# A copy inside SBUF in the first turn of GpSimd's DMA queue, and one DMA engine's rows spread in eighths

## Chip, cores and metric

The kernel runs on one core of one Trainium2 chip. The metric is the device time of one execution in microseconds (us); several executions of a kernel are given by their median, lowest and highest. A profiled execution also has a span, from its first to its last instruction. The core has a tensor engine (PE, which reads its weights as PEld), a vector engine (DVE), a scalar engine (ACT), GpSimd (POOL) and SyncE (SP), and 16 DMA engines, numbered 0 to 15 here. SP and POOL issue this kernel's transfers; SP's go through queue q1, POOL's through q0.

## The reference

```python
def reference(x, y):   # both (8, 12, 512, 64) float32
    return np.einsum('bhtc,bhsc->bhts', x, y).astype(np.float32)
```

For each of 96 pairs (batch, head) a 512 x 512 matrix is made as x times y transposed, over 64 channels. 25.17 MB are read and 100.66 MB written.

## The kernel before, in words

**Work and order.** The 96 pairs are taken in 6 groups of 16 (`NG`), each group in two halves (`NH` = 12). Inputs come in 2 MB loads (line 204), are turned into bf16 by ACT, DVE and POOL (lines 167 and 169), mixed into `xbs` (`mix`, line 232) and transposed in 32 x 32 blocks by DVE (`transposes`, lines 252 and 261). A half gives four *outputs* of 2 MB each (`V` = 4), 48 in all: 128 partitions of `N` = 4096 fp32 values, that is 16 KB a partition. In which order the four heads of a half are made is the list `heads` (line 157), here 0, 2, 1, 3; PE, ACT and the stores all follow it. For one output PE makes 8 products of 512 columns (line 275) into two PSUM tensors, ACT copies each to a slot in SBUF (line 167), and the slot is stored. Eight slots lie as four pairs.

**Stores.** Most stores take two outputs at once, 4 MB from a pair of slots, and are issued by SP (`store`, line 366, through `transfer`, line 184). Such a transfer is written as an access pattern of source and destination; the first count of the pattern is its outer one. SP issues each as soon as ACT has filled the slots, and the slots are filled again when the store has landed. The last output, 47, is copied out of PSUM by DVE.

**Output 44.** The first output of the last half (`SHARED` = 44) is stored in pieces. Its even partitions go with output 45's even ones in one 2 MB transfer of SP, output 45's odd ones in 1 MB behind it; outputs 46 and 47 are the last 4 MB of SP's queue. The odd partitions of output 44 are dealt out by `shares` (line 301). The code counts four partitions (so two odd rows) to a DMA engine in each of two blocks: with b = 0 or 1, engine e has the odd rows from 4e + 32b, for e above 7 from 32 more. `turns` (line 95) holds, as first engine and number of engines, (0, 5), (5, 3) and (8, 8). `odd` (line 304) issues the rows of k engines through `part` (line 293), which gives the source 2k rows and the destination the pattern (k, 2, columns).

- POOL issues, for b = 0 and then b = 1, the three turns. The rows of the first turn, engines 0 to 4, are cut: only columns 0 to `CUT[b]`, which are 512 (b = 0) and 1536 (b = 1) of the 4096; the others are whole.
- SP issues for engines 0 to 3 the columns from `CUT[b]` on, to the end with b = 0, to 1024 (`LEFT`) before the end with b = 1.
- What is left of these rows (of engine 4's, and the last 1024 columns of the rows of engines 0 to 4 with b = 1) is *made again*. `remade` (line 320) lists three pieces: columns 1536 to 3072 of engine 4's two rows of b = 1, cut in thirds for engines 13 to 15; the last 1024 columns of b = 1 of engines 0 to 4, whose ten rows lie on engines 8 to 12; and columns 512 to 4096 of engine 4's rows of b = 0 in eighths for engines 0 to 7. After its last product PE computes these pieces once more (`again`, line 330, matmuls on line 344), with the columns of the weights shifted so that a piece comes out on the partitions of the engines that are to store it; DVE copies them from PSUM to `xks[0]` and POOL issues three transfers (`rest`, line 351), in the order of their first engine.

So POOL's queue has, in this order, transfers with outer counts 5, 3, 8, 5, 3, 8 and, later, 8, 5, 3.

**Waits.** `emit` (line 140) gives every instruction the semaphore waits that its reads and writes need. Of POOL's transfers the first waits for ACT's copies of output 44, and the first of the made-again ones for DVE's copy.

Of the kernel before, what the change touches and what calls it, by code (L numbers as in the profile page):

```python
# [9 lines left out]
def kernel(  # L10
# [19 lines left out]
    _, _, S, _ = y.shape  # L30
    P = 128
# [10 lines left out]
    N = K * S  # L42
# [7 lines left out]
    while len(ROUNDS) < (V * NH - SINGLE) // 2:  # L50
        ROUNDS += [PAIRS - 1, *ROUND[LATE % 3:], *ROUND[:LATE % 3]]
    LAST = 2 * ROUNDS[(V * NH - SINGLE) // 2 - 1]
    CUT = [S, 3 * S]
    LEFT = 2 * S
    fp32 = mybir.dt.float32
    bf16 = mybir.dt.bfloat16
    u32 = mybir.dt.uint32
# [9 lines left out]
    def buffer(name, width, dtype):  # L67
        return nc.alloc_sbuf_tensor(name, [P, width], dtype)[:, :]
# [5 lines left out]
    def spare(g, lo, hi):  # L74

        return slots[SLOTS + g - 1][:, lo * N // 4:hi * N // 4]

    spares = range(1, 2 * PAIRS - SLOTS + 1)
    xks = [
        spare(g, 0, 2).bitcast(bf16) if g in spares else buffer(f"xk{g}", R * C, bf16)  # L80
        for g in range(NG - 1)
    ]
# [7 lines left out]
    xbs = [buffer(f"xb{half}", K * E * D, u32) for half in range(2)]  # L90
    xTs = [buffer(f"xT{i}", K * D * E, u32) for i in range(2)]
    yTs = [buffer(f"yT{i}", D * R // 2, u32) for i in range(2)]
    pms = [nc.alloc_psum_tensor(f"pm{i}", [P, 4, S], fp32)[:, :, :] for i in range(2)]

    turns = [(0, 5), (5, 3), (8, 8)]
    engines = {"act": nc.scalar, "dve": nc.vector, "pool": nc.gpsimd, "pe": nc.tensor, "sp": nc.sync}
# [3 lines left out]
    def need(name, points, told=True):  # L100

        best = {}
        for p, v in points:
            if known[name].get(p, 0) < v:
                best[p] = max(best.get(p, 0), v)
        for p, v in list(best.items()):
            if any(snaps[q, w].get(p, 0) >= v for q, w in best.items() if q != p):
                del best[p]
        for p, v in best.items():
            if told:  # L110
                engines[name].wait_ge(sems[p], v)  # L111
            known[name][p] = v
            for q, w in snaps[p, v].items():
                known[name][q] = max(known[name].get(q, 0), w)

    def promise(name, reads, writes):

        points = [writer[r] for r in (*reads, *writes) if r in writer]
        points += [v for w in writes for v in readers.get(w, ())]
        if name == "pool" and name in ticks:  # L120
            points.append((name, ticks[name]))
        return points

    def record(name, p, step, reads, writes, queue=False):
        at = (p, ticks.get(p, 0) + step)
        ticks[p] = at[1]
        if not queue:
            own[name][p] = at[1]
        snaps[at] = {**known[name], **own[name], p: at[1]}
        for r in reads:  # L130
            readers.setdefault(r, []).append(at)
        for w in writes:
            writer[w], readers[w] = at, []

    def signal(p):
        if p not in sems:
            sems[p] = nc.alloc_semaphore(p)
        return sems[p]

    def emit(name, make, reads=(), writes=(), dma=None, by=None, step=1):  # L140
        need(name, promise(name, reads, writes))
        p = by or name
        if dma is not None:
            p, step = f"dma{dma}", 16
        made = make().then_inc(signal(p), step)
        record(name, p, step, reads, writes, dma is not None)
        return made.ins.name
# [6 lines left out]

    places = [0, 4, 3, 1, 2, 0, 4, 3, 1, 2, 4, 3]
    first = [0, 1, 2, 4, 0, 1]
    heads = [0, 2, 1, 3]
    held = {
        SLOTS + g - 1: [[("xk", g)], [("yb", h, g, ch) for h in range(2) for ch in range(2)]]
        for g in spares  # L160
# [3 lines left out]
    def copy(name, dst, src, reads, writes, by=None):  # L164
        emit(
            name,
            lambda: nc.scalar.activation(dst, src, COPY)  # L167
            if name == "act"
            else engines[name].tensor_copy(dst, src),  # L169
            reads,  # L170
            writes,
            by=by,
        )

    def both(*ids):
        return [("slot", i, pm) for i in ids for pm in range(2)]

    def place(ap, pattern):
        name = ap.tensor.name
        return mybir.PhysicalAccessPattern(  # L180
            ap=pattern, offset=ap.offset, dtype=ap.dtype, memref=name, memsetref=f"{name}_set"
        )

    def transfer(name, dst, src, to=None, of=None):

        to = to or dst.ap
        of = of or [src.ap[0], *[[1, 1]] * (len(to) - len(src.ap)), *src.ap[1:]]
        return engines[name].add_instruction(  # L188
            mybir.InstDMACopy(
                name=nc.get_next_instruction_name(),  # L190
                engine=engines[name].engine,
                ins=[place(src, of)],
                outs=[place(dst, to)],
                mode="Copy",
                cce_op=mybir.AluOpType.bypass,
                queue={"sp": "qSPDynamicHW", "pool": "qPoolDynamic"}[name],
            )
        )
# [94 lines left out]
    def part(name, dst, src, k, reads, dma):  # L293

        assert src.ap[0][1] == 2 * k and dst.ap[0][1] == k
        emit(
            name, lambda: transfer(name, dst, src, dst.ap),
            reads=reads, dma=dma,
        )

    def shares(o, s):

        to, mine = ov[o // V, heads[o % V]], slots[s]
        def odd(name, b, e, k, lo, hi):

            p = 4 * e + 32 * b + (32 if e > 7 else 0)
            n = 2 * k
            dst = to[p // 2:p // 2 + n, 1, lo:hi].rearrange("(k i) n -> k i n", i=2)
            part(name, dst, mine[p + 1:p + 2 * n:2, lo:hi], k, both(s), "pool" if name == "pool" else s)

        for b in range(2):
            for e, k in turns:
                odd("pool", b, e, k, 0, N if e else CUT[b])
        for b in range(2):
            odd("sp", b, 0, 4, CUT[b], N - b * LEFT)

    remade = [  # L320
        (1, CUT[1], (N - LEFT - CUT[1]) // 3, 4, 13, 3, 0),
        (1, N - LEFT, LEFT, 20, 8, 5, 0),
        (0, CUT[0], (N - CUT[0]) // 8, 4, 0, 8, 0),
    ]

    def lies(e):

        return 4 * e + (32 if e > 7 else 0)
# [22 lines left out]
    def rest():  # L351

        half = SHARED // V % 2
        to = ov[SHARED // V, heads[SHARED % V]]
        top = lies(16)
        mine = xks[0][:top].bitcast(fp32)[:, :LEFT]
        emit("pe", again, [("xT", half), ("yT", half)], [("pm", 0)])
        copy("dve", mine, pms[0][:top, :LEFT // S].rearrange("p j s -> p (j s)"), [("pm", 0)], [("xk", 0)])
        for b, first, width, n, e, k, skip in sorted(remade, key=lambda r: r[4]):
            row, pieces = 16 * b + 10 - n // 2, 4 * k // n  # L360
            dst = to[row:row + n // 2, 1, first:first + pieces * width]
            dst = dst.rearrange("i (k n) -> k i n", k=k) if n == 4 else dst.rearrange("(k i) n -> k i n", k=k)
            p = lies(e)
            part("pool", dst, mine[p + 1:p + 4 * k:2, skip:skip + width], k, [("xk", 0)], "pool")

    def store(o):
        i, j = divmod(o, V)
        if o == SHARED:
            s = 2 * ROUNDS[(o - SINGLE) // 2]
            shares(o, s)  # L370
        elif o == SHARED + 1:
            n = ROUNDS[(o - SINGLE) // 2]
            emit(
                "sp", lambda: transfer("sp", ow[i, heads[j - 1]][:, :2], pairs[n][::2]),
                reads=both(2 * n, 2 * n + 1), dma=2 * n,
            )
            emit(
                "sp", lambda: transfer("sp", ov[i, heads[j]][:, 1], slots[2 * n + 1][1::2]),
                reads=both(2 * n + 1), dma=2 * n + 1,
            )  # L380
        elif o in ALONE:
            s = first[o]
            emit("sp", lambda: nc.sync.dma_start(ov[i, heads[j]], slots[s]), reads=both(s), dma=s)
        elif o % 2:
            n = first[o] // 2 if o < SINGLE else ROUNDS[(o - SINGLE) // 2]
            emit(
                "sp", lambda: transfer("sp", ow[i, heads[j - 1]], pairs[n]),
                reads=both(2 * n, 2 * n + 1), dma=2 * n,
            )
# [55 lines left out]
    for o in range(V, V * NH):  # L445
        result(o)
        if o % V == V - 1:
            prepare(o // V + 2)
    all_products()
    rest()  # L450
    emit("sp", nc.sync.nop)

# [35 lines left out]
```

## Time and profile before

| what | value |
|---|---|
| median of 3 runs | 297.85 us (297.57 to 297.97) |
| the profiled execution's own time | 298.19 us |
| its span | 296.4 us |
| PE, DVE, ACT, POOL busy | 45%, 53%, 69%, 22% of the span |
| moved by DMA, mean rate | 125.85 MB, 425 GB/s |
| landing of the last transfer | 296.29 us |

The profile is of one execution. Of its parts, the slices cut the span in 40 and give each engine's busy share in tenths; DMA in them is the mean of the 16 DMA engines. A line on DMA issues tells the destination and source, the issuing queue, how many, the size of each in KB and the median time from issue to landing. The trace under the page holds every DMA packet with its queue, start, length and size, but not its engine, and the moments at which each transfer's semaphore was incremented, 16 in all for a transfer. Each of a 4 MB transfer's packets is 32 KB, and an engine has eight of them.

### The profile page before, as it was taken

The numbers are of one execution on the slowest core, as the hardware profiler recorded it, in microseconds if no ns is written. First come the engines' busy times: TensorE is split into PE (matmuls) and PEld (weight loads), VectorE is DVE, ScalarE is ACT, GpSimd is POOL, SyncE is SP. The second block draws the span as 40 slices with busy tenths as digits, with TensorE's granted clock in tenths as the row PEclk, the third lists the DMA queues.
The fourth block names the chain that finished last, engine by engine and source line by source line (L and its number), as shares of the span: only waits on it lengthen the run. The fifth ranks groups of instructions, "written<-read, shape, count | busy, mean of one in ns | idle before, by whom it ended". The sixth has DMA issues, their size and how long they took to land.

```text
span 296.4 us, 1215 instructions
## 1 busy us (share of the span) xinstructions
PE 132.5 (45%) x397; PEld 36.5 (12%) x403; DVE 157.7 (53%) x76; ACT 205.5 (69%) x106; POOL 64.7 (22%) x33
## 2 busy tenths in 40 slices
PE   0000044434756455447555865546448655761000
PEld 0000011101211111111111211111111111121000
DVE  2167798896978681924908568772925100052000
ACT  1665669996999878667966999969666966640000
POOL 2399989997000000000000000000000000402000
PEclk9999999976799997897767699997895767677555
DMA  7999999999999999999999999999999999999996
GB/s 279 427 429 440 431 429 427 425 456 402 436 436 429 429 443 460 429 429 429 425 425 430 438 447 438 425 429 429 429 425 429 447 447 429 432 425 417 440 432 287
DMA packets 5898, 125.85 MB, mean 425 GB/s; under 512 B 936, under 2 KB 936, under 8 KB 980
## 3 DMA queue, kind: packets, MB, share of 16 engines
q1 hardware_dynamic: 5512, 124.95, 98.4%
q0 software_dynamic: 384, 0.89, 0.8%
q14 instruction: 2, 0.02, 0.0%
HBM read 25.17 MB, written 100.66 MB: 425 GB/s over the span
## 4 chain that ended last, share of the span: by engine, by line
DMA 59%; ACT 24%; PE 5%; issue 2%; DVE 1%; POOL 1%; SPq 0%; ACTq 0%
DMA out_dram<-room 46%; ACT room L167 22%; DMA room<-in_y_dram 7%; DMA room<-in_x_dram 6%; PE pm L275 4%; ACT xk L167 1%; PE pm L344 1%; DVE room L169 1%; POOL out_dram L188 1%; DVE xk L169 0%; SPq L204 0%; ACTq L111 0%
## 5 line engine op out<-in xcount | busy, mean ns | idle before, releaser
L167 ACT ACTIVATE room<-pm 128x2048 f32<-128x2048 f32 x94 | 170.2, 1891 | 37.2 <-DMA out_dram<-room 34.3
L275 PE MATMUL pm<-yT,xT 128*128 128x512 bf16 x378 | 129.5, 480 | 134.6 <-ACT room L167 96.6
L252 DVE STREAM_TRANSPOSE xT<-xb 128x2048 uint32<-128x2048 uint32 x12 | 46.7, 3889 | 59.7 <-PE pm L275 54.9
L275 PEld LDWEIGHTS pm<-yT,xT 128*128 128x128 bf16 x384 | 35.0, 112 | 228.7 <-ACT room L167 150.0
L188 POOL DMA_DIRECT2D out_dram<-room x6 | 3.5, 590 | 180.9 <-ACT room L167 180.9
L169 DVE COPY xb<-room 32x2048 bf16<-32x2048 bf16 x20 | 26.1, 1305 | 0.6
L167 ACT ACTIVATE room<-room 128x4096 bf16<-128x4096 f32 (+1 forms) x6 | 18.2, 3035 | 11.2 <-DMA room<-in_x_dram 7.3
L169 POOL COPY xb<-xk 32x2048 bf16<-32x2048 bf16 x8 | 23.6, 2948 | 6.9 <-ACT xk L167 6.5
L169 DVE CAST yb<-room 64x2048 bf16<-64x2048 f32 x6 | 17.1, 2857 | 9.6 <-DMA room<-in_y_dram 9.6
L169 DVE COPY room<-pm 128x2048 f32<-128x2048 f32 x2 | 4.5, 2285 | 31.9 <-PE pm L275 31.9
L169 DVE CAST room<-room 64x2048 bf16<-64x2048 f32 x6 | 19.1, 3179 | 4.1 <-DMA room<-in_y_dram 4.0
L169 DVE COPY xb<-xk 32x2048 bf16<-32x2048 bf16 x16 | 20.9, 1304 | 0.4
L167 ACT ACTIVATE xk<-room 128x4096 bf16<-128x4096 f32 x3 | 10.9, 3617 | 3.2 <-DMA room<-in_x_dram 3.2
L169 POOL CAST yb<-room 64x2048 bf16<-64x2048 f32 x4 | 12.7, 3173 | 0.5
L169 POOL COPY xb<-room 32x2048 bf16<-32x2048 bf16 x4 | 12.7, 3179 | 0.3
L261 DVE STREAM_TRANSPOSE yT<-yb 128x1024 uint32<-128x1024 uint32 x6 | 11.6, 1936 | 0.0
L261 DVE STREAM_TRANSPOSE yT<-room 128x1024 uint32<-128x1024 uint32 x6 | 11.5, 1919 | 0.0
L169 POOL CAST room<-room 64x2048 bf16<-64x2048 f32 x3 | 8.5, 2829 | 1.0 <-DMA room<-in_y_dram 0.7
L167 ACT ACTIVATE yb<-room 64x2048 bf16<-64x2048 f32 x2 | 4.9, 2459 | 1.3 <-DMA room<-in_y_dram 1.3
L188 POOL DMA_DIRECT2D out_dram<-xk x3 | 1.7, 572 | 13.1 <-DVE xk L169 13.1
L167 ACT ACT_TABLE_LOAD x1 | 1.3, 1283 | 4.2 <-PEq L420 4.2
L428 DVE MEMSET xb<- 128x2048 uint32 x1 | 1.8, 1765 | 4.6 <-PEq L420 4.6
(8 smaller groups left out, 7.8 us busy)
## 6 DMA issues: line engine op xcount, KB each, us to landing
out_dram<-room SPq DMA_DIRECT2D x21, 4096.0 KB, 23.3
room<-in_x_dram SPq DMA_DIRECT2D x6, 2048.0 KB, 17.9
room<-in_y_dram SPq DMA_DIRECT2D x6, 2048.0 KB, 20.8
out_dram<-room SPq DMA_DIRECT2D x5, 2048.0 KB, 12.1
out_dram<-room SPq DMA_DIRECT2D x1, 1024.0 KB, 29.4
out_dram<-room POOLq DMA_DIRECT2D x2, 256.0 KB, 18.4
out_dram<-room POOLq DMA_DIRECT2D x2, 96.0 KB, 16.4
out_dram<-room SPq DMA_DIRECT2D x1, 112.0 KB
```

The source lines that it names most:

```text
L167: lambda: nc.scalar.activation(dst, src, COPY)
L169: else engines[name].tensor_copy(dst, src),
L188: return engines[name].add_instruction(mybir.InstDMACopy(name=nc.get_next_instruction_name(), engine=engines[name].engine, ins=[place(src, ...
L252: lambda: nc.vector.transpose(xTs[half].rearrange("p (k r e) -> p k e r", k=K, e=E), xbs[half].rearrange("p (k e c) -> p k e c", k=K, e=E),),
L261: lambda: nc.vector.transpose(yTs[half].rearrange("p (r j) -> p j r", r=D), ybs[half][b].rearrange("p (j c) -> p j c", c=D),),
L275: last = nc.tensor.matmul(pms[k // 4][:, j, :], xT[:, k + j, h, :], yT[:, h * S:(h + 1) * S], start=True, stop=True,)
L344: last = nc.tensor.matmul(pms[0][:top, at // S, at % S:at % S + hi - lo], xT[:, stop - top:stop], yT[:, h * S + lo % S:h * S + lo % S + hi ...
L428: lambda: engines[name].memset(xbs[half], 0.0),
```

## The change

The rows of engines 0 to 4 are no longer in POOL's queue. In the place of the first turn POOL issues a copy inside SBUF, of 512 bytes in each of ten partitions, from `xbs[0]` to a new buffer `passed` that nothing reads. SP's two transfers for engines 0 to 3 take whole rows. All of engine 4's rows are made again: those of b = 0 in eighths for engines 0 to 7, those of b = 1 in eighths for engines 8 to 15, so 16 matmuls of 512 columns, half as many columns in DVE's copy, and two transfers of POOL instead of three. `heads` becomes 1, 3, 0, 2: the slice of the weights in `again` begins before the columns of a head, which needs a head in front of output 44's.

```diff
-    CUT = [S, 3 * S]
-    LEFT = 2 * S
...
+    passed = buffer("passed", 2 * P, u32)
...
-    heads = [0, 2, 1, 3]
+    heads = [1, 3, 0, 2]
...
-        def odd(name, b, e, k, lo, hi):
+        def odd(name, b, e, k, hi=N):
...
-            dst = to[p // 2:p // 2 + n, 1, lo:hi].rearrange("(k i) n -> k i n", i=2)
-            part(name, dst, mine[p + 1:p + 2 * n:2, lo:hi], k, both(s), "pool" if name == "pool" else s)
+            dst = to[p // 2:p // 2 + n, 1, :hi].rearrange("(k i) n -> k i n", i=2)
+            part(name, dst, mine[p + 1:p + 2 * n:2, :hi], k, both(s), "pool" if name == "pool" else s)
 
         for b in range(2):
             for e, k in turns:
-                odd("pool", b, e, k, 0, N if e else CUT[b])
+                if e:
+                    odd("pool", b, e, k)
+                else:
+                    emit(
+                        "pool", lambda: transfer("pool", passed[:2 * k, P * b:P * (b + 1)], xbs[0][:2 * k, :P]),
+                        [("xb", 0, 0)], [("passed", b)], "pool",
+                    )
         for b in range(2):
-            odd("sp", b, 0, 4, CUT[b], N - b * LEFT)
+            odd("sp", b, 0, 4)
...
-    remade = [
-        (1, CUT[1], (N - LEFT - CUT[1]) // 3, 4, 13, 3, 0),
-        (1, N - LEFT, LEFT, 20, 8, 5, 0),
-        (0, CUT[0], (N - CUT[0]) // 8, 4, 0, 8, 0),
-    ]
+    remade = [(1, 0, N // 8, 4, 8, 8, 0), (0, 0, N // 8, 4, 0, 8, 0)]
...
-        mine = xks[0][:top].bitcast(fp32)[:, :LEFT]
+        mine = xks[0][:top].bitcast(fp32)[:, :S]
...
-        copy("dve", mine, pms[0][:top, :LEFT // S].rearrange("p j s -> p (j s)"), [("pm", 0)], [("xk", 0)])
+        copy("dve", mine, pms[0][:top, :1].rearrange("p j s -> p (j s)"), [("pm", 0)], [("xk", 0)])
```

## The prediction

> **What bounds the kernel now.** I read the page's slices and DMA queues first, then the chain that ended last, then the last microseconds, then the issues of the stretch that the change touches. The page:
>
> ```profile
> DMA  7999999999999999999999999999999999999996
> ...
> q1 hardware_dynamic: 5512, 124.95, 98.4%
> q0 software_dynamic: 384, 0.89, 0.8%
> ...
> DMA 59%; ACT 24%; PE 5%; issue 2%; DVE 1%; POOL 1%; SPq 0%; ACTq 0%
> ```
>
> The sixteen DMA engines are full in every slice but the first and the last; 98.4% of their time goes to SP's queue (q1), 0.8% to GpSimd's (q0). No engine's own row comes near that, so the time is the bytes of the busiest DMA engine over its rate. The end shows which one. Stretches of the span: length, busy time of five engines, granted clock, DMA share, GB/s.
>
> ```profile
> 292.00:293.00 1.00, 0.00 (x0) 0.00 (x0) 0.00 (x0) 0.00 (x0) 0.00 (x0) 0.50 1.14 492
> ...
> 294.60:296.40 1.80, 0.00 (x0) 0.00 (x0) 0.00 (x0) 0.00 (x0) 0.00 (x0) 0.50 0.05 18
> ```
>
> 18 GB/s for 1.80 us is 32 KB: one packet of one DMA engine, alone. In the trace's packets a new one starts 3 to 4 ns before the last of its engine ends, so they can be strung together into engines. Fifteen strings end at 294.38 to 294.77 us, one at 295.83, and the last landing (296.29) follows that one. In the tail the late string holds GpSimd's 4,096- and 6,144-byte packets, which five strings have, and none of SP's 14,336- and 6,144-byte ones, which four of those five have: it is the fifth engine. It lags because many of its 32 KB packets take 1.23 to 1.25 us where the others take 1.213; the sixteenth increment of a 4 MB transfer came 0.9 us after the fifteenth at 121 us and 2.4 us after it at 259 us. The kernel already spares this engine bytes, and it is still 1.06 us behind the next.
>
> **How GpSimd's transfers fall on engines.** The issues from 252 to 258 us (size, time to landing):
>
> ```profile
> out_dram<-room POOLq DMA_DIRECT2D x2, 256.0 KB, 18.4
> out_dram<-room POOLq DMA_DIRECT2D x2, 96.0 KB, 16.4
> out_dram<-room SPq DMA_DIRECT2D x1, 112.0 KB
> out_dram<-room POOLq DMA_DIRECT2D x1, 60.0 KB, 17.1
> out_dram<-room SPq DMA_DIRECT2D x1, 48.0 KB
> out_dram<-room POOLq DMA_DIRECT2D x1, 20.0 KB, 8.0
> ```
>
> The trace gives each issue's pattern: outer count 5 for the 20 and 60 KB ones, 3 for the 96 KB ones, 8 for the 256 KB ones. The 20 KB are five packets of 4,096 bytes on five strings, the 60 KB ten packets on the same five, the 96 KB six packets on three others. So two rows hold here: **an issue uses as many engines as its outer count**, and **the next issue goes on where the last stopped** (5 + 3 + 8 = 16, and the second round starts at the first engine again).
>
> **The change, part by part.** In KB per engine, from the code: the odd rows of output 44 are 1 MB, 64 KB on each engine if nothing is moved. Before: engines 0-3 carry 59.5 (16 from GpSimd's turns, 40 from SP, 3.5 made again), engine 4 19.5 (16 + 3.5), 5-7 67.5, 8-12 72, 13-15 68. All else is equal on all sixteen.
>
> *Meant.* If the copy takes five engines, the turns stay as they are: engine 4 carries one 4 KB packet, all others 68 KB.
>
> *As it is written.* `passed[:2 * k]` and `xbs[0][:2 * k, :P]` are patterns of 10 rows of 512 bytes on both sides: the outer count is 10, not 5 (`part` gives the destination k as its outer count; this call does not). By the rows above the copy then uses ten engines, and everything behind it moves by five: copy 0-9, three on 10-12, eight on 13-4, copy 5-14, three on 15-1, eight on 2-9, and the two made-again transfers on 10-1 and 2-9. Two 16 KB rows per engine and turn: engines 0-3 get 64 from GpSimd, 64 from SP and 4, so 132 KB; engines 4 and 15 get 64 + 4 = 68; the rest 36. The sum is 1,024 KB as it must be.
>
> The price per packet from this trace's tail: 16 KB 0.611 us, 14,336 bytes 0.535, SP's 6,144 0.238, GpSimd's 6,144 0.234, 4,096 0.159, 3,584 0.140. Engine 4 had 0.159 + 2 x 0.234 + 0.140 = 0.77 us and gets 4 x 0.611 + 0.159 = 2.60: +1.84, end 295.83 + 1.84 = 297.67. Engines 0-3 had 0.77 + 2 x 0.535 + 2 x 0.238 = 2.31 and get 8 x 0.611 + 0.159 = 5.05: +2.73 on ends between 294.56 and 294.75, so 297.3 to 297.5. **Engine 4 still ends last, 1.84 us later.**
>
> The Trainium skill has a rule that speaks against the change in the same way (DMA: Bandwidth & Descriptors, section "Why a DMA increments its semaphore by 16 and not by 1"): a copy uses the largest count up to 16 that divides the slowest dimensions of both sides, and one issued by GpSimd takes consecutive engines from a round-robin cursor. The trace's 5, 3 and 8 agree; for 10 rows it gives ten engines. It also tells of an exception, some GpSimd copies that use all sixteen; then the cursor would not move, the turns would be three on 0-2, eight on 3-10, three on 11-13, eight on 14-5, and engine 4 would again carry 68 KB. No run here shows either for this copy.
>
> *The rest costs nothing on the path.* Each copy moves 5 KB, at most 0.1 us on an engine. The first waits only for a mixing copy of VectorE that ended near 194 us, and POOL idles from 72 to 253; the data turns behind it go out one issue (0.57 us) sooner, the second round's as before. SP issues two instructions as before, only larger. The made-again matmuls become 16 of 512 columns: at 379 to 417 ns for such a row that is about 6.2 us against the 2.9 of now; the copy out of PSUM halves from 1.22 us (-0.6), and one of three issues goes (0.57). So these rows reach the queue some 2.7 us later, near 272.5 instead of 269.6:
>
> ```profile
> 265.17 2.91 PE L344 MATMUL pm<-yT,xT 128*96 128x512 bf16 x19 [1.01 <-DVE room L169]
> ...
> 268.11 1.22 DVE L169 COPY xk<-pm 96x1024 f32<-96x1024 f32 x1 [0.81 <-PE pm L344]
> 269.63 1.71 POOL L188 DMA_DIRECT2D out_dram<-xk  x3 [13.14 <-DVE xk L169]
> ```
>
> The cover is the backlog: the made-again rows land by 284.83 now, and SP's last 4 MB, issued at 267.34, 29 us after their issue, so the former would have to be some 11 us late to count. If that cover were gone, the 2.7 us would. The order of heads changes addresses, no size.
>
> *Unknown.* Off their turns, engines read rows of partitions that another engine is reading. No row shows two on one group of partitions. Lower bound nothing (the packets of a shape differ by a few per cent all along); upper bound, each such 16 KB packet takes twice its time: 4 x 0.611 = 2.44 us more on engine 4. Nothing excludes either; I take nothing, by the nearest rows, the one-row-in-two transfers of output 45, whose 16 KB packets keep to 0.611 to 0.631.
>
> Sum: 298.19 (profiled; span 296.4, 1.8 around it) + 1.84 = 300.03. The median of the runs, 297.85, is 0.34 below the profiled one; the difference carries over: **299.7**.
>
> **Rivals.**
> 1. *Faster: the copy takes five engines after all.* For it: only that the two rows per engine of every other turn would be kept; against it, the outer count. Engine 4 then has 0.159 and two small copy packets: -0.5 to -0.6, end 295.3. Engines 0-3 have 4 x 0.611 + 0.159 = 2.60 against 2.31: +0.29, so 294.9 to 295.1, next in line. Gain 0.4 to 0.6: 297.4.
> 2. *No gain with five engines.* The median lies 0.34 under the profiled run; if in timed runs the fifth engine is not late at all, engines 0-3 decide and lose 0.29: 298.1. Against it: 0.34 is a third of the 1.06 it lags.
> 3. *Much slower: ten engines and shared partitions.* The upper bound above: 297.85 + 1.84 + 2.44 = 302.1. It decides as soon as two engines on one group of partitions are served in turn.
>
> **Chances.** Forecast 0.48, rival 1 0.34, rival 2 0.08, rival 3 0.10. A measurement of this kernel tells about 0.2% (0.6 us) from no change. Rival 1 lies just inside this: of its 0.34 I give 0.13 to faster, 0.19 to same, 0.02 to slower; rival 2 is same. Faster 0.13, same 0.27, slower 0.60. The forecast's own range is 299.3 to 300.6 (the upper end: in timed runs engines 0-3 decide, +2.73). Cases of both signs hold most of the chance, so the range for all reaches from rival 1 to there, 297.2 to 300.6, and leaves out most of rival 3 and the tails.
>
> **What would show it.** Right: each copy leaves ten packets of 512 bytes on ten engines; in the last two microseconds about five engines are at work, a DMA share near 0.3, not 0.05; the span near 298.2. Five packets of 1,024 bytes or two per engine on five engines, the last packet near 295.3 and ends that lie together would show rival 1. 16 KB packets of GpSimd's queue well over 0.7 us would show rival 3. The forecast is wrong if the copy is split otherwise than its outer count says, or if timed runs have another late engine.

## The result and the profile after

The changed kernel takes 300.48 us (median of 5 runs, 300.38 to 300.8), the kernel before 297.57 us (5 runs, 297.42 to 297.97): a ratio of 1.0096, 95% interval 1.0082 to 1.011, slower by about 2.9 us. The profiled execution has 300.48 us and a span of 298.6.

The page of the changed kernel, slices, queues and chain:

```profile
DMA  7999999999999999999999999999999999999996
...
q1 hardware_dynamic: 5512, 125.05, 98.1%
q0 software_dynamic: 320, 0.80, 0.9%
...
DMA 58%; ACT 23%; PE 6%; issue 2%; DVE 1%; POOL 0%; SPq 0%; ACTq 0%
```

Hardly anything in the shares has moved: the bound is the same, DMA engines that are full in every slice but the first and the last. What differs stands in two stretches. The end of the changed kernel (columns: stretch, length, busy time of the five engines, granted clock, DMA share, GB/s):

```profile
292.00:293.00 1.00, 0.00 (x0) 0.00 (x0) 0.00 (x0) 0.00 (x0) 0.00 (x0) 0.50 0.99 426
294.60:296.40 1.80, 0.00 (x0) 0.00 (x0) 0.00 (x0) 0.00 (x0) 0.00 (x0) 0.50 0.47 200
296.40:298.60 2.20, 0.00 (x0) 0.00 (x0) 0.00 (x0) 0.00 (x0) 0.00 (x0) 0.50 0.14 60
```

Before, one engine was at work from 294.6 us on (18 GB/s). Now it is about half of them, and after 296.4 four more packets of 32 KB begin (60 GB/s for 2.2 us is 132 KB). In the strings of packets (the packets of one engine, each starting as the last one ends) these are mainly the four with SP's whole rows, so engines 0 to 3; where two engines end a packet at the same moment a string can't be followed with certainty. The four last strings end at 297.65, 297.82, 298.04 and 298.21 us. The fifth engine ends at 297.42.

The second stretch is the one in which GpSimd's transfers run. It is the second line here, below the 20 us before it:

```profile
236.00:256.00 20.00, 12.32 (x35) 3.15 (x34) 0.00 (x0) 14.94 (x9) 2.82 (x5) 0.74 0.99 428
256.00:276.00 20.00, 8.28 (x28) 2.64 (x28) 5.17 (x3) 3.65 (x2) 1.12 (x2) 0.77 1.01 396
```

The kernel before had in the second of these stretches:

```profile
256.00:276.00 20.00, 7.89 (x33) 2.70 (x31) 5.71 (x3) 4.17 (x3) 2.20 (x4) 0.76 0.99 423
```

In the changed kernel the engines are as busy in its second line as in its first (1.01 against 0.99) and move less (396 against 428 GB/s). A full engine that moves less has longer packets: between 256 and 276 us, 18 of 43 of GpSimd's 16 KB packets take more than 0.8 us, up to 1.39 where 0.611 is the rule, and 22 of SP's 32 KB packets more than 1.58 us, up to 2.06 where 1.213 is the rule. In the kernel before there is none of either.

The issues around it, and the copy out of PSUM:

```profile
193.94 1.14 POOL L187 DMA_DIRECT2D passed<-xb  x1 [122.21 <-DVE xb L168]
252.36 1.15 POOL L187 DMA_DIRECT2D out_dram<-room  x2 [57.28 <-ACT room L166]
253.50 0.54 POOL L187 DMA_DIRECT2D passed<-xb  x1
254.03 1.14 POOL L187 DMA_DIRECT2D out_dram<-room  x2
...
264.43 3.76 PE L345 MATMUL pm<-yT,xT 128*96 128x512 bf16 x16 [0.75 <-DVE room L168]
268.23 0.69 DVE L168 COPY xk<-pm 96x512 f32<-96x512 f32 x1 [1.65 <-PE pm L345]
269.21 1.12 POOL L187 DMA_DIRECT2D out_dram<-xk  x2 [14.04 <-DVE xk L168]
```

The first copy is issued alone at 194 us, the second between the two rounds of turns; the made-again rows are issued at 269.21, where before it was 269.63. Each copy leaves ten packets of 512 bytes, of 0.027 us each; those of the first lie on ten strings. So the copies do use ten engines. Whether they also move the turns, that is, the engine at which the next transfer of the queue starts, is another matter, and the first experiments are about it.

### The profile page after: what moved, and what is told of

It reads as the page before. It is cut to its first block, busy times and chain, and to the rows that moved or that the text cites. A ratio compares the mean times of both kernels' runs of the same rounds, so it can differ in the third digit from the quotient of the medians.

```text
span 298.6 us, 1214 instructions
## 1 busy us (share of the span) xinstructions
PE 138.5 (46%) x400; PEld 37.1 (12%) x400; DVE 157.1 (53%) x76; ACT 205.7 (69%) x106; POOL 64.5 (22%) x32
## 4 chain that ended last, share of the span: by engine, by line
DMA 58%; ACT 23%; PE 6%; issue 2%; DVE 1%; POOL 0%; SPq 0%; ACTq 0%
DMA out_dram<-room 45%; ACT room L166 22%; DMA room<-in_y_dram 7%; DMA room<-in_x_dram 6%; PE pm L274 4%; PE pm L345 1%; ACT xk L166 1%; DVE room L168 1%; POOL out_dram L187 0%; SPq L203 0%; DVE xk L168 0%; ACTq L110 0%
## 5 line engine op out<-in xcount | busy, mean ns | idle before, releaser
L274 PE MATMUL pm<-yT,xT 128*128 128x512 bf16 x384 | 134.8, 495 | 128.9 <-ACT room L166 92.0
L274 PEld LDWEIGHTS pm<-yT,xT 128*128 128x128 bf16 x384 | 35.6, 113 | 227.3 <-ACT room L166 147.5
L187 POOL DMA_DIRECT2D passed<-xb x2 | 1.7, 844 | 122.2 <-DVE xb L168 122.2
L187 POOL DMA_DIRECT2D out_dram<-room x4 | 2.3, 573 | 57.3 <-ACT room L166 57.3
```

Of the source, the lines that this page charges most:

```text
L187: return engines[name].add_instruction(mybir.InstDMACopy(name=nc.get_next_instruction_name(), engine=engines[name].engine, ins=[place(src, ...
L274: last = nc.tensor.matmul(pms[k // 4][:, j, :], xT[:, k + j, h, :], yT[:, h * S:(h + 1) * S], start=True, stop=True,)
```

## The experiments

Every kernel was timed beside the kernel before on the same chip, but not all on one chip. Ratios with their 95% intervals (the code cuts below are shortened, and it is said which kernel each is against):

| kernel | median us (range) | ratio to the kernel before | span us |
|---|---|---|---|
| changed kernel | 300.48 (300.38 to 300.8) | 1.0096 (1.0082 to 1.011) | 298.6 |
| e1, copies of 5 rows | 300.31 (300.18 to 300.38) | 1.0087 (1.0073 to 1.0101) | 298.5 |
| e2, copies of 10 and 11 rows | 300.87 (300.8 to 301.01) | 1.0107 (1.0092 to 1.0123) | 299.0 |
| e3, whole rows, copy of 16 rows | 298.98 (298.91 to 299.38) | 1.0042 (1.0027 to 1.0058) | 297.5 |
| e4, whole rows, copy of 8 rows | 299.02 (298.95 to 299.03) | 1.0044 (1.0029 to 1.0059) | 297.2 |
| e5, copy in the form (5, 2, 128) | 297.42 (297.38 to 297.66) | 0.9996 (0.9987 to 1.0005) | 295.6 |
| e6, no copy | 300.02 (299.96 to 300.1) | 1.0083 (1.0068 to 1.0098) | 298.2 |
| e7, whole rows, copy in the form (8, 2, 128) | 300.7 (300.58 to 300.83) | 1.0104 (1.0089 to 1.012) | 299.0 |
| e8, only the order of heads | 297.62 (297.49 to 297.99) | 1.0002 (0.9993 to 1.0011) | 295.8 |
| e9, form (5, 2, 128) on both sides | 297.5 (297.32 to 298.05) | 1.0 (0.999 to 1.0009) | 295.5 |
| e10, e5 and 64 KB more on engines 0-3 | 300.07 (299.99 to 300.2) | 1.0084 (1.0067 to 1.01) | 298.3 |
| e11, without SP's rows | 299.66 (299.61 to 299.73) | 1.0071 (1.0054 to 1.0087) | 297.8 |

**Do the copies move the turns by their rows?** If they did, two kernels (e1 and e2) should put the turns back; of two others with whole rows one (e3) should leave every row on its own engine and one (e4) should swap the halves.

e1, from the changed kernel:

```diff
-  transfer("pool", passed[:2 * k, P * b:P * (b + 1)], xbs[0][:2 * k, :P])
+  transfer("pool", passed[:k, P * b:P * (b + 1)], xbs[0][:k, :P])
```

> The changed kernel with one thing altered: each copy inside SBUF has 5 rows of 512 bytes instead of 10. Theory (a copy takes as many engines as its outer count, and with ten the later turns fall on the wrong engines): ten packets of 512 bytes in all, every 16 KB packet of GpSimd's queue at 0.61 to 0.67 us again, no 32 KB packet above 1.35 us after 256 us, and 0.0 to 0.6 us under the kernel before, so about 297.3, some 3.1 us under the changed kernel. Rival (the copies themselves, SP's whole rows or the order of heads cost the time): all of these stay, so about 300.5.

Measured 300.31: the rival's number. Five packets of 512 bytes a copy, as the theory had it, but again 18 of 43 of GpSimd's 16 KB packets between 256 and 276 us take more than 0.8 us. The copy takes as many engines as it has rows and yet the turns are where the changed kernel has them.

e2, also from the changed kernel:

```diff
+                    for c, rows in enumerate((10, 11)):
+                        at = P * (2 * b + c)
...
+                            "pool", lambda: transfer("pool", passed[:rows, at:at + P], xbs[0][:rows, :P]),
```

> The changed kernel with a second copy, of 11 rows, behind each copy of 10 rows: the two together move the turns by 21, which is 5 beyond a full round of 16. Theory (only where the next turn starts matters, not that the copies use ten engines): the turns are back, the time is that of the kernel with 5 rows, about 297.3, within 0.3 us, with two more copies in the queue. Rival (the copies cost by their number, or by using ten engines): at or above the changed kernel, 300.5 or more. If the count of engines were not the outer count for 10 or 11 rows, the turns would fall somewhere else and GpSimd's 16 KB packets would again take up to 1.3 us.

Measured 300.87, with long packets. The theory fails a second time: 21 rows bring nothing back.

e3 (`n` = 16) and e4 (`n` = 8), from the changed kernel; they have no made-again rows and no rows by SP:

```diff
+        emit(
+            "pool", lambda: transfer("pool", passed[:n, :P], xbs[0][:n, :P]),
+            [("xb", 0, 0)], [("passed", 0)], "pool",
+        )
         for b in range(2):
-            for e, k in turns:
...
-            odd("sp", b, 0, 4)
+            for e in (0, 8):
+                odd("pool", b, e, 8)
...
-    rest()
```

> All odd rows of output 44 by GpSimd, whole, in turns of eight engines (0-7, 8-15, twice), 64 KB on every engine, nothing by SP and nothing made again; in front of them one copy inside SBUF of 16 rows, which moves the turns by a full round. Theory: each engine reads its own rows, GpSimd's 16 KB packets take 0.61 to 0.67 us, and the fifth engine, spared nothing, ends about 4 x 0.61 - 0.77 = 1.7 us later than in the kernel before: 299.2, between 298.4 and 299.6. Rival (the fifth engine's lag doesn't set the end of unprofiled runs): at most 0.3 us over the kernel before, 297.9. It is the base for the next kernel.

> The same, but the copy in front has 8 rows, so that every turn falls on the other eight engines: each engine still has 64 KB, but all of them from the rows of an engine of the other half. Theory (two engines that read one group of partitions share its rate, so each such 16 KB packet costs about 0.6 us to one of the two): 64 such packets over 16 engines, 4 x 0.61 = 2.4 us later than the same kernel with its own rows, so about 301.6, with packets of GpSimd's queue near 1.2 us and 32 KB packets near 1.8 us. Rival (only the load of the engines counts): the same time as the kernel with its own rows, 299.2, and no packets longer than there.

Measured 298.98 and 299.02. e3 is near its number: the fifth engine, spared nothing, lands at 297.44 us, 2.3 us after the next. e4 is equal to it, without one long packet. That is the rival's number, but it says nothing on sharing if a copy of 8 rows doesn't move the turns; it fits e1 and e2. So the first theory has fallen: **a plain copy of rows, of 5, 8, 10, 16 or 10 + 11, leaves the turns where they are.** In the changed kernel they start at the first engine: three on 0-2, eight on 3-10, three on 11-13, eight on 14-5. Its strings agree: two of the four with SP's rows take one of GpSimd's 16 KB packets at 257.07 and 257.60 us, the first of all, where the forecast had engines 10 to 12.

**What does move them?**

e5, from the changed kernel, with the copy in the form of the other transfers:

```diff
-  transfer("pool", passed[:2 * k, P * b:P * (b + 1)], xbs[0][:2 * k, :P])
+  to5 = passed[:k, 2 * P * b:2 * P * (b + 1)].rearrange("k (i n) -> k i n", i=2)
+  part("pool", to5, xbs[0][:2 * k, :P], k, [("xb", 0, 0)], "pool")
```

> The changed kernel, but the copy is written in the form of the other transfers of GpSimd's queue: source of 10 rows, destination of 5 rows with two runs of 512 bytes each, so the destination's pattern is (5, 2, 128) and not a plain one of rows. My first theory (a plain copy of n rows moves the turns by n) has fallen: copies of 5, 8, 10, 16 and 10 + 11 rows all left the turns where they were. Second theory: a plain copy of rows puts a row on an engine from the first on and leaves the turns at the first engine, while a transfer in this form takes k engines and moves the turns by k. Then here the turns are back: no 16 KB packet of GpSimd's queue over 0.70 us, no 32 KB packet over 1.35 us after 256 us, and 297.1 to 297.7. Rival (what decides is that the copy stays inside SBUF; such copies never move the turns): 300.3, packets as in the changed kernel. Rival (SP's whole rows on engines 0 to 3 cost the time): no long packets, yet 298.5 or more.

Measured 297.42, five packets of 1,024 bytes a copy, the longest 16 KB packet of GpSimd's queue 0.634 us. The turns are back, and 3.06 us with them. The stretch of 256 to 276 us and the end of e5:

```profile
256.00:276.00 20.00, 8.06 (x28) 2.78 (x28) 5.27 (x3) 3.76 (x3) 1.13 (x2) 0.81 1.01 431
294.60:296.40 1.80, 0.00 (x0) 0.00 (x0) 0.00 (x0) 0.00 (x0) 0.00 (x0) 0.50 0.00 0
```

Same DMA share as in the changed kernel, 431 instead of 396 GB/s, and no packet of 32 KB begins after 294.6 us. This is the change with the turns left in place, as it was meant: its time is that of the kernel before, within the interval.

e9 asks which part of the form counts (against e5):

```diff
-  part("pool", to5, xbs[0][:2 * k, :P], k, [("xb", 0, 0)], "pool")
+  of5 = xbs[0][:k, :2 * P].rearrange("k (i n) -> k i n", i=2)
+  transfer("pool", to5, of5, to5.ap, of5.ap)
```

> The kernel with the copy in the form (5, 2, 128), but now on both sides, from 5 rows to 5 rows, where it had 10 rows on the source's side. It tells what in the form counts. If it is that the pattern has one more level than plain rows: the turns are moved as there, about 297.4, no long packets. If it is that source and destination have a different number of rows (10 and 5): the copy counts as a plain one of rows, the turns start at the first engine, about 300.3 with 16 KB packets up to 1.4 us.

Measured 297.5, five packets of 1,024 bytes: the turns are moved. So it is not a different number of rows on the two sides, and not that the copy stays in SBUF. What is left is the extra level of the pattern, or what came with it: two runs of 512 bytes a row, so 1,024 bytes on an engine, where the plain copies have 512. A plain copy with rows of 1,024 bytes was not run, so which of the two counts, and why, is not shown.

e6 takes the copies away from the changed kernel:

```diff
-                else:
-                    emit(
-                        "pool", lambda: transfer("pool", passed[:2 * k, P * b:P * (b + 1)], xbs[0][:2 * k, :P]),
```

> The changed kernel without the copies inside SBUF: GpSimd's queue holds 3, 8, 3, 8 and the two made-again transfers. Second theory (the plain copies move nothing): the same turns as in the changed kernel, the same long packets, 300.2 to 300.5. First theory (the copies move the turns by 10): the turns would then fall on other engines, though with as many bytes on engines 0 to 4: also near 300, but engines 10 to 12 would lose their first packets, so the four engines with SP's whole rows would show their first 16 KB packets of GpSimd's queue later than 260 us in three of four strings in the one case and at 257 to 258 us in three strings in the other.

Measured 300.02, with long packets (32 KB up to 2.37 us): without any copy the turns are still those of the changed kernel. Of the early packets, two that are on strings with SP's rows (257.55 and 257.97 us) speak for turns from the first engine; the third (258.16) is on a string that can't be followed to the end, so the test by strings is not complete. The time is 0.46 us below the changed kernel's, and e2, with two copies more, 0.39 above it: that would be about 0.2 us for each plain copy. It is not shown: e6 and e2 ran on different chips, and the intervals of the three ratios overlap. Their packets alone (0.027 us on an engine) would not explain it.

**What does it cost that the turns are wrong?** Two things can: 64 KB more on engines 0 to 3, and *foreign* packets, that is, rows of partitions that another engine is reading.

e7 has equal loads and swapped halves, now with a copy that does move the turns (against e4, and run on another chip):

```diff
-            "pool", lambda: transfer("pool", passed[:8, :P], xbs[0][:8, :P]),
+        to8 = passed[:8].rearrange("k (i n) -> k i n", i=2)
+        part("pool", to8, xbs[0][:16, :P], 8, [("xb", 0, 0)], "pool")
```

> The kernel with whole rows in turns of eight, 64 KB on every engine, but the copy in front has the form (8, 2, 128), which by the second theory moves the turns by 8, so that each engine reads the rows of an engine of the other half. Theory that engines share the rate of a group of partitions: all 64 packets of GpSimd's queue or their partners get longer, in all by some 64 x 0.61 = 39 us of engine time, 2.4 us an engine, so 301.4 against 299.0 for own rows. Rival (the load alone made the changed kernel slower, and the long packets there have another cause): 299.0 and packets at 0.61 and 1.21 us. If the copy doesn't move the turns in this form either, also 299.0, and the kernel with five rows in this form shows it.

Measured 300.7 against 298.98 and 299.02 with the same load on own rows. The stretch of 256 to 276 us, first of e3, then of e7:

```profile
256.00:276.00 20.00, 4.91 (x13) 1.18 (x12) 4.49 (x2) 3.93 (x3) 0.00 (x0) 0.58 1.00 431
```

```profile
256.00:276.00 20.00, 4.37 (x12) 1.05 (x12) 4.50 (x2) 3.91 (x3) 0.00 (x0) 0.71 1.01 365
```

As busy, and 66 GB/s less. 39 of GpSimd's 64 packets take more than 0.8 us, up to 1.49, and 33 of SP's more than 1.58, up to 2.00. Counting all 64 over 0.611 us and all of SP's 32 KB packets of the stretch over 1.213 us, 51 us of engine time are lost, 0.8 us for each of the 64, about half of it on GpSimd's packets and half on SP's; in e3 it is 0.1 us. So two engines that read one group of partitions do slow each other. The end moves by 1.7 us and not by 51/16 = 3.2, since in e3 only the fifth engine set it: its landing goes from 297.44 to 298.92 at most, the other fifteen from 294.5-295.2 to 297.2-298.6.

e10 has the load without the sharing (against e5, with e5's copy):

```diff
         for b in range(2):
             odd("sp", b, 0, 4)
+        for c, dead in enumerate((xTs[0], xbs[1])):
+            for j in range(4):
+                src = mine[j:16:4, c * N // 2:(c + 1) * N // 2]
+                emit("sp", lambda: transfer("sp", dead.bitcast(fp32)[j:16:4], src), reads=both(s), dma=s)
```

> The kernel with the turns in place, the copy of form (5, 2, 128) from 10 rows, plus eight copies inside SBUF on SP's queue, of four rows of 8 KB each, from output 44's own rows of engines 0 to 3 to dead buffers on the same partitions: 64 KB more on engines 0 to 3, as the changed kernel gives them, with nobody reading another engine's partitions. Theory (load of the first four decides, sharing adds a little): 4 x 0.61 = 2.4 us over the kernel it is made from, 299.9, no long packets in GpSimd's queue; what the changed kernel has above that, about 0.5 us, is the sharing. Rival (sharing is the main part): under 298.5.

Measured 300.07, 2.65 us over e5 and 2.57 over e9, which ran on the same chip (2.44 forecast; the eight packets of 8 KB on each of the four engines take 0.313 us each, 2.50 together). Its stretch and its end:

```profile
256.00:276.00 20.00, 8.38 (x29) 2.70 (x28) 5.17 (x3) 3.81 (x3) 1.13 (x2) 0.84 1.00 429
294.60:296.40 1.80, 0.00 (x0) 0.00 (x0) 0.00 (x0) 0.00 (x0) 0.00 (x0) 0.50 0.30 127
```

429 GB/s and no long packet: no sharing. And only a few engines at the end: twelve of the last transfer's sixteen increments come by 295.37 us, the other four at 297.52 to 298.28. What the changed kernel has beyond this, 0.4 us, is left for sharing and the two plain copies together. e6, with the sharing and without copies, takes 300.02, no longer than e10, so it is open whether sharing adds anything to the end of these kernels, though it lowers the rate (396 and 399 GB/s in the changed kernel and e6).

e11, from the changed kernel, has the sharing and leaves SP's rows out:

```diff
-        for b in range(2):
-            odd("sp", b, 0, 4)
```

> The changed kernel without SP's two transfers of the rows of engines 0 to 3, so it leaves those rows of output 44 out. GpSimd's turns fall as in the changed kernel and share partitions, but engines 0 to 3 carry 68 KB, not 132. Theory: the first four end 4 x 0.61 = 2.4 us earlier, the fifth engine, with its 68 KB, decides at the 297.4 us of the packets that it had in the changed kernel's profile, 0.8 us before that kernel's end: 299.7, between 299.0 and 300.0. Rival (the sharing on whatever engine decides): no change from 300.4.

Measured 299.66, as the theory said. Without SP's rows the last landing is 0.8 us earlier (297.77 against 298.54), not 2.4, since another engine is next in line: the last string ends at 297.41, where the fifth engine's ended at 297.42.

e8 tests one of the edits that I had put at nothing (against the kernel before):

```diff
-    heads = [0, 2, 1, 3]
+    heads = [1, 3, 0, 2]
```

> The kernel before with nothing but the new order of heads, 1, 3, 0, 2. Forecast: the order changes addresses in memory and no size, so the time of the kernel before, within 0.3 us. Rival (the order of the addresses that the last stores write matters): up to 1 us of difference, seen in the durations of the 32 KB packets after 256 us.

Measured 297.62, no difference. Its profile is of use in another way: the stores are those of the kernel before, and its last landing is at 295.71 us, only 0.49 us after the next, where the profiled execution of the kernel before had 296.29 and 1.13.

## Why the prediction was right, and where it was not

The direction, the bound and the range were right: 300.48 lies between 299.3 and 300.6. But the time rose by 2.9 us and not by 1.84, and two steps under the forecast of 299.7 were wrong; that one of them left the sum as it was is luck.

- **What bounds the kernel: right.** The time is the bytes of the busiest DMA engine over its rate. Putting 64 KB on four engines costs 2.65 us (e10), and taking the wrong turns away gives 3.06 back (e5).
- **"The next issue goes on where the last stopped": wrong for this copy.** The step took a row that held for patterns of three levels and applied it to a plain one. The copy does use ten engines, as forecast, but moves nothing (e1, e2, e4, e6). The loads of engines 0 to 4 are the same by either count, 132 KB on the first four and 68 on the fifth, so the sum came through unhurt: luck, not insight. The sign that the prediction gave for being right, ten packets on ten engines, could not tell the two cases apart. The prediction had the better case at hand. The Trainium skill (DMA: Bandwidth & Descriptors, "Why a DMA increments its semaphore by 16 and not by 1") tells of an exception, some GpSimd copies that count as using all sixteen engines; from this the prediction had worked out that the cursor would not move. The runs agree with it as far as the turns go. A copy of 10 rows leaves data packets on ten strings only, one each, which is what that section's rows per engine would give as well. The 4-byte packets that follow lie on all sixteen strings, but e5's copy leaves them there too, so they decide nothing.
- **"Engine 4 still ends last, 1.84 us later": wrong.** Engines 0 to 3 end last, at 297.65 to 298.21, where the sum had 297.3 to 297.5, and the fifth engine ends at 297.42, where it had 297.67. For the first four the load is not what was wrong: with the same 132 KB and no sharing (e10) the last four landings come at 297.52 to 298.28, and in the changed kernel at 297.99 to 298.54; the difference is the 0.4 us that sharing and copies have together. For the fifth the error is in the start: I added 1.84 to the end that it had in one profiled execution. Its lag isn't a constant. In the changed kernel's execution it was 0.8 us less late near 258 us and yet ended only 0.25 under its number; foreign packets may have taken up the rest, which is not shown. At the landing near 258 us the sixteenth increment came 2.44 us after the fifteenth in that execution, 1.61 in the changed kernel's, 2.04 in e8's, 2.73 in e3's; and that execution, 298.19 us, lies above all the other runs of its kernel (297.31 to 298.0). Where the fifth engine is only half a microsecond late, as in e8's execution (297.6 us, like the timed runs), the first four pass it. The prediction named this as the upper end of its own range, 300.6.
- **"I take nothing" for shared partitions: wrong for the packets, open for the time.** A foreign 16 KB packet costs 0.8 us of engine time (e7), even more than the 0.611 of the upper bound; of the 300.48 at most 0.4 us are due to it (e10), and perhaps nothing (e6). So the sign of rival 3, long packets, was there without its price, 302.1. The rows that I called nearest, output 45's, say nothing on the question.
- **The copies cost "at most 0.1 us on an engine": open.** It may be about 0.2 us of the time each, with the caution given at e6.
- **The made-again products: hidden, as forecast, but mis-sized.** I multiplied 16 by the 379 to 417 ns of one matmul and had 6.2 us; the 16 took 3.76. Matmuls overlap, so a row's own duration is no price: the 19 before took 2.91 us together, at a median of 0.30 us each.
- **Rival 1's gain of 0.4 to 0.6 us was too large.** With the turns in place (e5, e9) the time is 0.9996 and 1.0 of the kernel before. It rested on the fifth engine's lag in the same execution; where that is half as large, engines 0 to 3, with 8.5 KB more, take most of the gain. In e5's trace the last string, ending at 295.21 us, is one with SP's whole rows.

## What to carry to other kernels

When several engines run full to the end, price a change on every engine that it loads, and start from the lag that an engine has in many executions, not from the one that happened to be profiled. A transfer that is there only for its place in a round-robin is best given the form of the transfers around it; the packets that it leaves show how many engines it used, but only the next transfer's packets show where the turn went. When the DMA share stays and the GB/s fall, packets have become longer, and two engines on one group of partitions are a reason to look for.

## What the runs showed that I had not expected

- A GpSimd copy of plain rows leaves the next transfer's first engine unchanged, whatever its number of rows (5, 8, 10, 16, or 10 and 11 in two copies); with one more level in the pattern, and with it two runs of 512 bytes a row, (5, 2, 128) or (8, 2, 128), the same queue moves on by 5 or 8, and with 5 it does so whether the source has as many rows or twice as many.
- Two DMA engines that read the same partitions at once slow each other: 431 GB/s became 365 at the same DMA share when all of GpSimd's rows were foreign, 396 in the changed kernel.
- One DMA engine is behind the others in every run; that it is the fifth shows in the packets of the kernel before. Its lag at about 258 us, after nearly the same work, was between 1.57 (e11) and 2.73 us (e3) in the profiled executions; e3, which spares it nothing, ends 1.3 us later than the kernel before for it (298.98 against 297.67 on the same chip).
